# Seven-product groups for branch B's queries and keys and six gate tiles of the long sequence, in a stage of their own

## The chip, the cores and the metric

One core of one Trainium2 chip. The metric is the time of one execution on the device in microseconds (us); lower is better. The engines are PE (matmul), DVE (vector), ACT (scalar), POOL (GpSimd) and SP, which here only issues loads.

## The reference

One encoder layer on two sequences, `x_sample` (512 tokens, trunk 0) and `x_prompt` (1024 tokens, trunk 1), with a model width of 1024 and float32 throughout:

```python
xn = rmsnorm(x);  z = xn @ w_in       # q_A | k_A | v_A | q_B | k_B | v_B | gate_A | gate_B
o_A = grouped-query attention(q_A, k_A, v_A)      # 8 heads over 2 key heads, rotary, every key
o_B = neighbourhood attention(q_B, k_B, v_B)      # 8 heads, window of at most 8 x 16 on a grid 64 wide, bias
mix = (sigmoid(gate_A) * (o_A @ w_proj_a) + sigmoid(gate_B) * (o_B @ w_proj_b)) @ w_out
x = x + mix
x = x + relu(rmsnorm(x) @ w_mlp_up)**2 @ w_mlp_down
y = rmsnorm(x)
```

`w_in` has 4352 columns. Columns 768 to 1279 are q_B, 1280 to 1791 k_B, 2304 to 3327 gate_A, 3328 to 4351 gate_B.

## The kernel before

**Precision.** Every float32 product is made of three matmuls on pairs of rounded parts (`mm3`, lines 190 to 193: high x high, low x high, high x low). So each matrix that feeds PE is first split: ACT writes the high part (`hi = copy(src)`), DVE the low part (`lo = src - hi`). One product with a depth of 1024, a 128-wide weight and 512 tokens takes 8 x 3 = 24 matmuls of 128x512.

**Stages.** `run` handles a trunk: trunk 0 first, then trunk 1 with twice the tokens (`NB` = 2 blocks `tb` of 512 tokens). For each of two key-head groups g there is a stage R (norm, q/k/v of branch A, rotary) and a stage A (attention over all keys). Then branch B makes its attention (stage B), stage G merges, and after both trunks the MLP runs for all tokens. The MLP's up-projection already uses seven-product groups (tiles `ua`, `ub`, `uc`, `ud`; helper lines 1184 to 1304).

**Stage A of trunk 1** runs over 8 units (head, half of the queries) and 8 key chunks `kc`. Per chunk: four transposes into `pTs` (L722), ACT copies them to `pths` (L727), DVE subtracts into `ptls` (L728), and two chunks later PE multiplies both with the values into `os` (L698, L699). In chunks 0, 1, 3 and 4 a score tile `ss` of the next unit (L679, L680) is made: DVE takes its maximum (L682), ACT the exponential (L685), DVE the reciprocal of the sum (L687), and POOL scales (L688).

**Filling.** `gate` makes the gate tiles: a generator of steps of one `mm3` (three matmuls into `gpss`), with a weight split per tile (ACT L180, DVE L186). `fill.pull(n)` puts n such steps into the PE stream. In stage A of trunk 1 six of eight chunks pull one step; `fill.drain()` at the end of each g places what is left. Gate A's tiles 0 to 3 belong to g = 0, tiles 4 to 7 to g = 1. Gate B's eight tiles fill stage B.

**Branch B of trunk 1.** For each pair of heads `qkproj` multiplies q and k (PE `pqbs`, `pkbs`; 4 pairs x 2 x 2 tb x 24 matmuls) and writes the split results into `qBs` and `kBs` (ACT L836 and L854, DVE L838 and L856, half the partitions at a time). There are 32 units: `s_unit` (scores `sbs`, L888; POOL adds bias `rects` and mask `msks` to `bms`, L874; one DVE operation adds and takes the minimum, L891; ACT exponential, L896; DVE reciprocal, L898; POOL scale, L899), one unit later `t_unit` (transposes `ptbs`, L911; ACT `bhs`, L916; DVE `bls`, L917), another unit later `v_unit` (`obs`, L932). Up to unit 23 five or six fill steps stand in each unit; in the last eight, seven steps of the output projection of A (`ppas`).

**What sets the order.** A list scheduler places the instructions of each engine in program order as far as its costs allow, and it may move independent ones forward; each engine then runs its list in order and waits on semaphores. SBUF comes from pools: `slot` (long-lived), `rawp` (3 buffers for raw loads), and a pool per stage. PSUM tiles come from `mm` (one bank) and `big` (two).

Of the kernel before, what the change touches and what calls it, by code (L numbers as in the profile page):

```python
# [11 lines left out]
F32 = mybir.dt.float32  # L12
# [6 lines left out]
P = 128  # L19
# [42 lines left out]
def encoder(ctx: ExitStack, tc: tile.TileContext, xs, outs, w):  # L62
# [21 lines left out]
    def phase(name, bufs=2):  # L84
        return tc.tile_pool(name=name, bufs=bufs, reuse_waits="tile")
# [293 lines left out]
    def run(tr, nxt, first):  # L379
# [89 lines left out]
        def load_v(g, alloc, pin=False):  # L469
            return load_cols(win, 1792 + 256 * g, 256, f"v{N}_{g}", alloc, pin)  # L470

        early = {}
        for g in range(2):
            with phase(f"phR{N}_{g}") as ph:
                xn_of = {}
                fresh = g == 0 and tr.ready < NT
# [105 lines left out]
                for tt in range(NT):  # L582
# [67 lines left out]
                    if first and g == 0 and tt == 1:  # L650
                        load_pad()
                    if tt == NT - 2:
                        fill.add(gate(2304, zg[0], g * 4, g * 4 + 4))
                        fill.pull(1)

                if g == 0:
# [10 lines left out]
            with phase(f"phA{N}_{g}") as ph:  # L667
# [41 lines left out]
                for ui, u in enumerate(units):  # L709
                    h, qb = u  # L710
                    if first:
                        bias_row(g * 4 + ui)
                        if g == 0 and ui == 1:
                            early["a"] = load_a(1)
                        if g == 0 and ui == 2:
                            early["v"] = load_v(1, slot)
                    nxt_u = units[ui + 1] if ui + 1 < len(units) else None
                    sdone = 0
                    for kc in range(NT):
                        pt = mm(f"pT{N}_{g}_{h}_{qb}_{kc}")  # L720
                        for j in range(4):
                            nc.tensor.transpose(  # L722
                                pt[:, j * P : (j + 1) * P], PP[u, j][:, kc * P : (kc + 1) * P], ident
                            )
                        hi = ph.tile([P, 512], F32R, tag="pth", name=f"pth{N}_{g}_{h}_{qb}_{kc}", bufs=3)
                        lo = ph.tile([P, 512], F32R, tag="ptl", name=f"ptl{N}_{g}_{h}_{qb}_{kc}", bufs=3)
                        nc.scalar.activation(hi, pt, AF.Copy)  # L727
                        nc.vector.tensor_tensor(lo, pt, hi.bitcast(F32), op=ALU.subtract)  # L728
# [12 lines left out]

        mA = {}
        wp_b = []
# [44 lines left out]
        with phase(f"phB{N}") as ph:  # L788
# [24 lines left out]
            def qkproj(pr, wqk, dest):  # L813
# [4 lines left out]
                for tb in range(NB):  # L818
# [31 lines left out]
                    for e in range(2):  # L850
# [4 lines left out]
                        for os_ in (hs, ls):  # L855
                            nc.vector.tensor_tensor(  # L856
                                kT[e][os_, 1, cs], pk[hs], kT[e][hs, 0, cs].bitcast(F32), op=ALU.subtract
                            )

            qk = {}  # L860
            def s_unit(u):
                h, j = u
# [85 lines left out]
                    finish_o(o, nq, None, ph, f"B{nm}", (hi, lo, ps))  # L948

            prep(0)  # L950
            fill.add(gate(3328, zg[1]))
            wqk = load_qk(0)
            fill.pull(1)
            for _ in qkproj(0, wqk, qk):
                pass
            units = [(h, j) for h in range(8) for j in (1, 2, 0, 3)]
            n = len(units)
            LS, LV = (1, 1) if NB == 2 else (2, 1)
            qp = None
            for i in range(n + LS + LV):  # L960
                if i < n - 8:
                    f = (5 if i < LS else 2 + i % 2) if NB == 1 else 5 + (i % 3 > 0)
                else:
                    f = 3 + i % 2 if NB == 1 else 7
                if i < n:
                    s_unit(units[i])
                    if units[i][1] == 1 and units[i][0] + 1 < 8:
                        prep(units[i][0] + 1)
                    if i % 8 == 6 and i + 2 < n:
# [19 lines left out]
                if i == 3:  # L989
                    wqk = load_qk(1)  # L990
                if qp is not None and NB == 2:
                    for _ in range(NC8):
                        next(qp)
# [713 lines left out]
```

## Time and profile before

| | |
|---|---|
| three runs | 2174.45, 2174.66, 2172.08 us; median 2174.45 us |
| span of the profiled execution | 2172.2 us |
| PE busy | 2135.6 us, 98% |
| DVE, ACT, POOL busy | 1456.1, 1109.3, 349.4 us (67%, 51%, 16%) |
| granted TensorE clock | nine tenths or more in all 40 slices |

The profile has a row per group of instructions and a timeline of each. A matmul's row is longer than its share of PE's time, since matmuls overlap: the step from one start to the next is its price. Times such as 662.7 are from the start of the span. Trunk 1 stands in it as follows: stage A of g = 0 from 470.7 to 599.7, stage R to 662.7, stage A of g = 1 to 791.4, first q/k and gates to 814.6, branch B to 1094.1, stage G to 1232. Trunk 0's stage A of g = 0 is at 56.1 to 97.8 and its branch B at 186 to 293; the MLP's up-projection begins at 1238.

### The profile page before, as it was taken

The numbers are of one execution on the slowest core, as the hardware profiler recorded it, in microseconds if no ns is written. First come the engines' busy times: TensorE is split into PE (matmuls) and PEld (weight loads), VectorE is DVE, ScalarE is ACT, GpSimd is POOL, SyncE is SP. The second block draws the span as 40 slices with busy tenths as digits, with TensorE's granted clock in tenths as the row PEclk, the third lists the DMA queues.
The fourth block names the chain that finished last, engine by engine and source line by source line (L and its number), as shares of the span: only waits on it lengthen the run. The fifth ranks groups of instructions, "written<-read, shape, count | busy, mean of one in ns | idle before, by whom it ended". The sixth has DMA issues, their size and how long they took to land. (4 is left out here: it accounts for less than half of the span.)

```text
span 2172.2 us, 32392 instructions
## 1 busy us (share of the span) xinstructions
PE 2135.6 (98%) x11162; PEld 1867.9 (86%) x11162; DVE 1456.1 (67%) x2837; ACT 1109.3 (51%) x2379; POOL 349.4 (16%) x458
## 2 busy tenths in 40 slices
PE   8999999999999999999999999999999999999998
PEld 7788778888898888888888899998999988888886
DVE  6675566777756754555772777778777777769663
ACT  5654553556645744545531466656556643433452
POOL 2232210433233313322300200003000000000000
PEclk9999999999999999999999999999999999999999
DMA  5436457620122132423464656568544799788551
GB/s 166 144 104 179 137 145 249 211 71 28 45 75 86 44 92 88 125 80 110 136 195 137 202 180 195 179 226 223 158 156 155 234 347 343 224 268 290 175 194 68
DMA packets 319773, 350.94 MB, mean 162 GB/s; under 512 B 31352, under 2 KB 255224, under 8 KB 319609
## 3 DMA queue, kind: packets, MB, share of 16 engines
q1 hardware_dynamic: 277927, 279.65, 41.4%
q10 hardware_dynamic: 36002, 52.19, 6.9%
q0 software_dynamic: 5680, 17.04, 2.7%
q8 instruction: 88, 1.44, 0.3%
q14 instruction: 76, 0.62, 0.1%
HBM read 264.85 MB, written 87.88 MB: 162 GB/s over the span
## 5 line engine op out<-in xcount | busy, mean ns | idle before, releaser
L192 PE MATMUL dn<-wd,ah 128*128 128x512 f32 x624 | 243.0, 389 | 0.0
L193 PE MATMUL dn<-wd,al 128*128 128x512 f32 x624 | 243.0, 389 | 0.0
L191 PE MATMUL dn<-wd,ah 128*128 128x512 f32 x624 | 243.0, 389 | 0.0
L1184 ACT ACTIVATE ah<-ar 128x512 fp32r<-128x512 f32 x168 | 103.9, 627 | 195.1 <-PE dn L192 176.8
L1185 DVE TENSOR_TENSOR al<-ar,ah 128x512 fp32r<-128x512 f32 x168 | 115.1, 693 | 73.9 <-ACT ah L1184 66.7
L192 PEld LDWEIGHTS dn<-wd,ah 128*128 128x128 f32 x624 | 117.2, 188 | 24.4
L193 PEld LDWEIGHTS dn<-wd,al 128*128 128x128 f32 x624 | 117.2, 188 | 24.2
L191 PEld LDWEIGHTS dn<-wd,ah 128*128 128x128 f32 x624 | 117.2, 188 | 24.1
L728 DVE TENSOR_TENSOR ptls<-pTs,pths 128x512 fp32r<-128x512 f32 x160 | 107.7, 686 | 37.9 <-ACT pths L727 37.0
L727 ACT ACTIVATE pths<-pTs 128x512 fp32r<-128x512 f32 x160 | 94.1, 597 | 74.0 <-PE pTs L722 71.8
L688 POOL TENSOR_SCALAR ps<-ps,rls 128x1024 f32<-128x1024 f32 (+1 forms) x96 | 96.6, 1007 | 216.2 <-DVE rls L687 197.2
L682 DVE TENSOR_REDUCE nms<-ss 128x1 f32<-128x1024 f32 (+1 forms) x96 | 99.9, 1041 | 25.4 <-PE ss L680 25.0
L191 PE MATMUL gpss<-xs_0h,w_gs 128*128 128x512 f32 x256 | 106.2, 415 | 0.8 <-DVE rlbs L898 0.7
L685 ACT ACTIVATE ps<-ss,nms 128x1024 f32<-128x1024 f32 (+1 forms) x96 | 93.2, 972 | 22.4 <-DVE nms L682 20.0
L722 PEld LDWEIGHTS pTs<-ident,ps 128*128 128x128 f32 x640 | 78.2, 140 | 28.1 <-POOL ps L688 4.2
L193 PE MATMUL gpss<-xs_0h,w_gs 128*128 128x512 f32 x256 | 101.7, 397 | 0.0
L192 PE MATMUL gpss<-xs_0l,w_gs 128*128 128x512 f32 x256 | 101.6, 397 | 0.0
L722 PE MATMUL pTs<-ident,ps 128*128 128x128 f32 x640 | 98.9, 274 | 1.3 <-DVE ptls L728 0.6
L176 POOL TENSOR_TENSOR rs_f<-ms_f,mhalf 128x1 f32<-128x1 f32 x6 | 4.0, 667 | 590.7 <-DVE ms_f L172 590.7
L1184 ACT ACTIVATE A<-S 128x512 fp32r<-128x512 f32 x128 | 75.9, 623 | 29.4 <-DVE S L1247 22.1
L891 DVE CUSTOM_DVE_ANT_0 sbss<-sbs,bms 128x384 f32<-128x384 f32 (+1 forms) x96 | 48.6, 508 | 58.2 <-issue 34.1
L191 PE MATMUL ud<-B,A 128*128 128x384 f32 x256 | 85.8, 335 | 1.4 <-DVE c L1302 1.4
(325 smaller groups left out, 6444.8 us busy)
## 6 DMA issues: line engine op xcount, KB each, us to landing
ar<-ud SPq DMA_DIRECT2D x120, 512.0 KB
br<-in_w_mlp_down_dram SPq DMA_DIRECT2D x72, 512.0 KB
rawu<-in_w_mlp_up_dram SPq DMA_DIRECT2D x64, 512.0 KB
ud<-c ACTq DMA_DIRECT2D x128, 192.0 KB
raw_gs<-in_w_in_dram SPq DMA_DIRECT2D x32, 512.0 KB
zgs<-sgs ACTq DMA_DIRECT2D x48, 256.0 KB
ud<-cs SPq DMA_DIRECT2D x64, 192.0 KB
raw_os<-in_w_out_dram SPq DMA_DIRECT2D x16, 512.0 KB
```

The lines of the kernel that those rows point to most:

```text
L191: nc.tensor.matmul(out, ah, bh, start=start, stop=False, **kw)
L192: nc.tensor.matmul(out, ah, bl, start=False, stop=False, **kw)
L193: nc.tensor.matmul(out, al, bh, start=False, stop=stop, **kw)
L682: nc.vector.tensor_reduce(nm_, s, axis=AX.X, op=ALU.max, negate=True)
L685: nc.scalar.activation(p, s, AF.Exp, bias=nm_, accum_out=l)
L688: nc.gpsimd.tensor_scalar(p, p, rl, 1.0, op0=ALU.mult, op1=ALU.mult)
L722: nc.tensor.transpose(pt[:, j * P : (j + 1) * P], PP[u, j][:, kc * P : (kc + 1) * P], ident)
L727: nc.scalar.activation(hi, pt, AF.Copy)
L728: nc.vector.tensor_tensor(lo, pt, hi.bitcast(F32), op=ALU.subtract)
L891: nc.vector.tensor_tensor_reduce(out=sb, in0=so, in1=bm, op0=ALU.add, op1=ALU.min, scale=-1.0, scalar=3e38, accum_out=nm_)
L1184: nc.scalar.activation(hi, src, AF.Copy)
L1185: nc.vector.tensor_tensor(lo, src, hi.bitcast(F32), op=ALU.subtract)
```

## The change

In trunk 1 seven pairs of column tiles leave the places where they were made: gate A's tiles 4 to 7, gate B's tiles 6 and 7, and the four pairs of heads each of q_B and k_B. Two tiles (256 columns) of q_B or k_B, or of a gate, times 1024 tokens and a depth of 1024 form one group: a 2x2 block product that is made with seven block products instead of eight, which takes 7 x 4 x 3 = 84 matmuls of 128x512 instead of 8 x 4 x 3 = 96. With two groups of q_B, two of k_B and three of gates there are seven groups, run in a new stage S (`wide`, pool `phS`) between branch A and branch B.

- The token forms `XF` (four new ones, of 4 chunks of 128x512 each): two subtractions and an addition of high and low parts, then the split. One chunk takes POOL 2, DVE 2 and ACT 1 operations. `x_form_step` stands in stage A of g = 1, the rest in stage S.
- The weight forms (`forms`): four DVE additions or subtractions per group and seven splits (ACT and DVE), made during the group before.
- The outputs (`group`, `put`): DVE additions of the products in PSUM and SBUF; gates go through tanh to DRAM as before; q and k are split and written to DRAM (`qd`, `kd`), and `load_qkd` reads each pair back on SP's queue, 3 MB per pair (`qBs`, `kBs`), in halves of 64 partitions.
- Fill: stage A has gate A's tiles 0, 1 (g = 0) and 2, 3 and gate B's 0 (g = 1); two of eight chunks pull in g = 0, three of eight in g = 1, and what is left of g = 1 is drained at the head of stage S. Branch B has gate B's tiles 1 to 5: eight steps at its start, five per unit in the first three units, then two or three.

```diff
+        XF, x_todo = {}, []
...
+            def chunk(i, a, b, c):
+                if i not in XF:
+                    XF[i] = tuple(slot([P, 4, 512], F32R, f"xf{n_}{N}_{i}") for n_ in "hl")
+                hi, lo = (t[:, c, :] for t in XF[i])
+                (ah, al), (bh, bl) = ([t[:, c, :].bitcast(F32) for t in XF[n]] for n in (a, b))
+                de = rawp.tile([P, 2, 512], F32, tag="raw", name=f"xd{N}_{i}_{c}")
+                nc.gpsimd.tensor_tensor(de[:, 1], al, bl, op=ALU.subtract)
+                nc.vector.tensor_tensor(de[:, 0], ah, bh, op=ALU.subtract)
+                nc.gpsimd.tensor_tensor(de[:, 0], de[:, 0], de[:, 1], op=ALU.add)
+                nc.scalar.activation(hi, de[:, 0], AF.Copy)
+                nc.vector.tensor_tensor(lo, de[:, 0], hi.bitcast(F32), op=ALU.subtract)
+
+            for i, a, b in ((2, 7, 0), (1, 4, 2), (3, 4, 7), (6, 5, 1)):
+                x_todo.extend(partial(chunk, i, a, b, c) for c in range(4))
...
+        def wide(ph):
+
+            raws = {}
+            todo = [("g", 2304 + 512, 4, zg[0])]
+            todo += [(kind, off + 256 * i, 2 * i, dst) for i in range(2) for kind, off, dst in
+                     (("q", 768, qd), ("k", 1280, kd))]
+            todo += [("g", 2304 + 768, 6, zg[0]), ("g", 3328 + 768, 6, zg[1])]
...
+                def one(i):
+                    if i == 1:
+                        S[0], S[1] = st(f"S0{N}_{n}"), st(f"S1{N}_{n}")
+                        nc.vector.tensor_tensor(S[0], a21, a22, op=ALU.add)
+                        nc.vector.tensor_tensor(S[1], S[0], a11, op=ALU.subtract)
+                    if i == 3:
+                        nc.vector.tensor_tensor(a21, a11, a21, op=ALU.subtract)
+                    if i == 4:
+                        nc.vector.tensor_tensor(S[1], a12, S[1], op=ALU.subtract)
+                    src = {0: a11, 1: S.get(1), 2: S.get(0), 3: a21, 4: S.get(1), 5: a12, 6: a22}[i]
+                    t = kf([P, 2, 4, P], f"sa{N}_{n}_{i}")
+                    nc.scalar.activation(t[:, 0], src, AF.Copy)
+                    nc.vector.tensor_tensor(t[:, 1], src, t[:, 0].bitcast(F32), op=ALU.subtract)
+                    A[i] = t
...
+            def group(n, A, side):
...
+                def prod(out, i, more):
+                    for k in range(4):
+                        mm3(
+                            out, A[i][:, 0, k, :], A[i][:, 1, k, :], XF[i][0][:, k, :], XF[i][1][:, k, :],
+                            k == 0 and not more, k == 3, skip_group_check=True,
+                        )
+                    if side:
+                        for s in side.pop(0):
+                            s()
+
+                s1, s5 = k2(f"s1{N}_{n}"), k2(f"s5{N}_{n}")
+                prod(a, 0, False)
+                nc.scalar.activation(s1, a, AF.Copy)
+                if n == 0:
+                    prod(a, 5, True)
+                    put(n, 0, 0, a)
+                prod(bk, 1, False)
+                nc.vector.tensor_tensor(s1, bk, s1, op=ALU.add)
+                prod(c, 2, False)
+                nc.scalar.activation(s5, c, AF.Copy)
+                nc.vector.tensor_tensor(s5, s5, s1, op=ALU.add)
+                if n > 0:
+                    prod(d, 3, False)
+                    put(n, 1, 1, d, s5, s5)
+                prod(c, 4, True)
+                put(n, 0, 1, c, s1)
+                if n == 0:
+                    prod(d, 3, False)
+                    put(n, 1, 1, d, s5, s5)
+                prod(d, 6, True)
+                put(n, 1, 0, d, s1, s1)
+                if n > 0:
+                    prod(a, 5, True)
+                    put(n, 0, 0, a)
+
+            ask(0)
+            A = {}
+            side = forms(0, A)
+            while side or len(x_todo) > 4:
+                x_form_step()
+                for s in side[:2]:
+                    s()
+                side = side[2:]
+            ask(1)
+            fill.drain()
+            for n in range(len(todo)):
+                nA = {}
+                side = forms(n + 1, nA) if n + 1 < len(todo) else []
+                side = [[s] for s in side]
+                if n == 0:
+                    side = [[x_form_step] * 2, [x_form_step] * 2] + [[]] + side[:3] + [side[3] + side[4] + side[5] + side[6]]
+                group(n, A, side)
+                A = nA
+                ask(n + 2)
...
+            if g == 1 and NB == 2:
+                x_forms()
...
-                        fill.pull(1 if NB == 1 or kc % 4 < 3 else 0)
+                        fill.pull(1 if NB == 1 or kc % (4 - g) == 0 else 0)
+                        if NB == 2 and g == 1 and kc == 3 and ui >= 1:
+                            for _ in range(1 + (ui > 6)):
+                                x_form_step()
...
-                fill.drain()
+                if NB == 1 or g == 0:
+                    fill.drain()
...
+        if NB == 2:
+            with phase(f"phS{N}") as ph:
+                wide(ph)
...
+                hs = slice(64 * e, 64 * e + 64)
+                ls = slice(64 - 64 * e, 128 - 64 * e)
+                nc.sync.dma_start(qT[hs, e, :].bitcast(F32), qd[pr][hs, 0, :])
+                nc.sync.dma_start(qT[ls, e, :].bitcast(F32), qd[pr][hs, 1, :])
+                for os_ in (hs, ls):
+                    nc.sync.dma_start(kT[os_, :, :].bitcast(F32), kd[pr][hs, :, :])
...
+                load_qkd(0, qk, 0)
+                fill.add(gate(3328, zg[1], 1, 6))
+                fill.pull(1)
+                load_qkd(0, qk, 1)
+                fill.pull(7)
...
-                    f = (5 if i < LS else 2 + i % 2) if NB == 1 else 5 + (i % 3 > 0)
+                    f = (5 if i < LS else 2 + i % 2) if NB == 1 else (5 if i < 3 else 2 + (i % 5 < 4))
...
+                    if NB == 2:
+                        if i % 8 in (4, 7) and i + 4 < n:
+                            load_qkd(i // 8 + 1, qk, i % 8 // 7)
```

**PE in branch A of trunk 1, g = 0, head 1, between key chunks 5 and 6.** Names are those of the stage above; `gpss` is a gate step. Before:

```order
L722 MATMUL pTs_0_1_0_5_6188<-ident,ps_0_1_0_3_6009 128x128
L191 MATMUL gpss_2304_1_1_6032<-xs_1h_4989,w_gs_2304_1_5612 128x512
L192 MATMUL gpss_2304_1_1_6032<-xs_1l_4991,w_gs_2304_1_5612 128x512
L193 MATMUL gpss_2304_1_1_6032<-xs_1h_4989,w_gs_2304_1_5612 128x512
L698 MATMUL os_0_1_0_6134<-pths_0_1_0_3_6142,vhls_0_4783 128x512
L699 MATMUL os_0_1_0_6134<-ptls_0_1_0_3_6143,vhls_0_4783 128x512
L722 MATMUL pTs_0_1_0_6_6202<-ident,ps_0_1_0_0_5911 128x128
```

After (lines are shifted; L884, L885 and L908 are the former L698, L699 and L722):

```order
L908 MATMUL pTs_0_1_0_5_6156<-ident,ps_0_1_0_3_5993 128x128
L884 MATMUL os_0_1_0_6102<-pths_0_1_0_3_6110,vhls_0_4791 128x512
L885 MATMUL os_0_1_0_6102<-ptls_0_1_0_3_6111,vhls_0_4791 128x512
L908 MATMUL pTs_0_1_0_6_6167<-ident,ps_0_1_0_0_5900 128x128
L908 MATMUL pTs_0_1_0_6_6167<-ident,ps_0_1_0_1_5928 128x128
```

The gate step between the transposes of chunk 5 and the `os` matmuls of chunk 3 is gone, so the next transposes follow after two matmuls instead of five.

**DVE in branch A, g = 1, at the end of the first unit's key chunks.** `ptls`, `nms` (the maximum) and `rls` are the work of the unit; L914, L868 and L873 are the former L728, L682 and L687. Before:

```order
L728 TENSOR_TENSOR ptls_1_0_0_6_8072<-pTs_1_0_0_6_8066,pths_1_0_0_6_8071 128x512
L728 TENSOR_TENSOR ptls_1_0_0_7_8089<-pTs_1_0_0_7_8083,pths_1_0_0_7_8088 128x512
L728 TENSOR_TENSOR ptls_1_0_1_0_8100<-pTs_1_0_1_0_8094,pths_1_0_1_0_8099 128x512
L682 TENSOR_REDUCE nms_1_1_0_0_8108<-ss_1_1_0_0_8103 128x1
L728 TENSOR_TENSOR ptls_1_0_1_1_8127<-pTs_1_0_1_1_8121,pths_1_0_1_1_8126 128x512
L682 TENSOR_REDUCE nms_1_1_0_1_8135<-ss_1_1_0_1_8130 128x1
```

After, where `xds` is a difference of two token blocks and `xfls` the low part of a token form:

```order
L873 RECIPROCAL rls_1_0_1_3_7921<-ls_1_0_1_3_7919 128x1
L489 TENSOR_TENSOR xfls_1_8707<-xds_1_0_8708,xfhs_1_8706 128x512
L489 TENSOR_TENSOR xfls_1_8707<-xds_1_1_8876,xfhs_1_8706 128x512
L914 TENSOR_TENSOR ptls_1_0_0_7_7958<-pTs_1_0_0_7_7952,pths_1_0_0_7_7957 128x512
L868 TENSOR_REDUCE nms_1_1_0_0_7977<-ss_1_1_0_0_7972 128x1
L914 TENSOR_TENSOR ptls_1_0_1_0_7969<-pTs_1_0_1_0_7963,pths_1_0_1_0_7968 128x512
L486 TENSOR_TENSOR xds_1_2_8998<-xs_1h_4997,xfhs_2_8056 128x512
```

Three operations of the token forms (L486, L489) now stand among those of the unit.

**DVE at the head of stage S, first group.** `sas` is a weight form's low part, `S0s`/`S1s` sums of weight blocks, `wbs` a product in PSUM, `s1s` its sum. Nothing of the kind stood here before:

```order
L548 TENSOR_TENSOR sas_1_0_9258<-rawss_1_0_9129,sas_1_0_9258 128x512
L486 TENSOR_TENSOR xds_6_0_9193<-xs_0h_4561,xfhs_1_8706 128x512
L613 TENSOR_TENSOR s1s_0_9177<-wbs_0_9174,s1s_0_9177 128x512
L489 TENSOR_TENSOR xfls_6_9192<-xds_6_0_9193,xfhs_6_9191 128x512
L539 TENSOR_TENSOR S0s_1_9275<-rawss_1_0_9129,rawss_1_1_9131 128x512
L486 TENSOR_TENSOR xds_6_1_9199<-xs_0h_4561,xfhs_1_8706 128x512
L540 TENSOR_TENSOR S1s_1_9276<-S0s_1_9275,rawss_1_0_9129 128x512
L542 TENSOR_TENSOR rawss_1_0_9129<-rawss_1_0_9129 128x4x128
L616 TENSOR_TENSOR s5s_0_9178<-s5s_0_9178,s1s_0_9177 128x512
L489 TENSOR_TENSOR xfls_6_9192<-xds_6_1_9199,xfhs_6_9191 128x512
```

The addition from `wbs` (L613) waits for PE's second product, and token form 6 (`xds_6`, `xfls_6`) stands behind it in DVE's list.

**SP's queue at the entry of branch B.** `rects` is the bias tile of a head, `raw_bqs`, `raw_bks` and `raw_gs` are raw weights, `vss` values. Before:

```order
L216 DMA raw_bks_0_0_9265<-in_w_in_dram 128x8x128
L216 DMA raw_gs_3328_0_0_9271<-in_w_in_dram 128x8x128
L216 DMA raw_gs_3328_1_0_9462<-in_w_in_dram 128x8x128
L216 DMA raw_gs_3328_2_0_9602<-in_w_in_dram 128x8x128
L216 DMA raw_bqs_1_0_9670<-in_w_in_dram 128x8x128
L795 DMA rects_0_9240<-biases 128x768
L795 DMA rects_1_9443<-biases 128x768
```

After, `qBs` and `kBs` are read back from `qds` and `kds`:

```order
L1066 DMA kBs_0_0_10210<-kds_0_4741 64x2048 x2
L1063 DMA qBs_0_10209<-qds_0_4737 64x1024
L1064 DMA qBs_0_10209<-qds_0_4737 64x1024
L1066 DMA kBs_0_1_10221<-kds_0_4741 64x2048 x2
L989 DMA rects_0_10190<-biases 128x768
L989 DMA rects_1_10281<-biases 128x768
L995 DMA vss_1_10283<-vds_4732 32x4x128 x16
```

The two bias tiles now stand behind the read-back of the first pair's q and k.

More of the change, by code (lines that the diff above doesn't have):

```diff
@@ L652, in run @@
                     if tt == NT - 2:
-                        fill.add(gate(2304, zg[0], g * 4, g * 4 + 4))
+                        if NB == 1:
+                            fill.add(gate(2304, zg[0], g * 4, g * 4 + 4))
+                        else:
+                            fill.add(gate(2304, zg[0], g * 2, g * 2 + 2))
+                            if g == 1:
+                                fill.add(gate(3328, zg[1], 0, 1))
                         fill.pull(1)
@@ L950, in run @@
             prep(0)
[L951 to L955, printed above, removed]
+            if NB == 1:
+                fill.add(gate(3328, zg[1]))
+                wqk = load_qk(0)
+                fill.pull(1)
+                for _ in qkproj(0, wqk, qk):
+                    pass
+            else:
+                load_qkd(0, qk, 0)
+                fill.add(gate(3328, zg[1], 1, 6))
+                fill.pull(1)
+                load_qkd(0, qk, 1)
+                fill.pull(7)
             units = [(h, j) for h in range(8) for j in (1, 2, 0, 3)]
@@ L988, in run @@
                     fill.add(pa)
-                if i == 3:
+                if i == 3 and NB == 1:
                     wqk = load_qk(1)
-                if qp is not None and NB == 2:
-                    for _ in range(NC8):
-                        next(qp)
                 fill.pull(f - f // 2)
```

79 lines of the change are left out of this document (78 added, 1 removed).

## The prediction

> **What bounds the kernel now.** I read the page first: busy shares, then the slices.
>
> ```profile
> span 2172.2 us, 32392 instructions
> ...
> PE 2135.6 (98%) x11162; PEld 1867.9 (86%) x11162; DVE 1456.1 (67%) x2837; ACT 1109.3 (51%) x2379; POOL 349.4 (16%) x458
> ...
> PE   8999999999999999999999999999999999999998
> ...
> DVE  6675566777756754555772777778777777769663
> ...
> PEclk9999999999999999999999999999999999999999
> ```
>
> PE has work for 98% of the span in every slice, at a clock of nine tenths or more. So the time is PE's list, and a change pays what it removes there less the gaps that it opens. Next I asked for the busy times by stage, to see how near the other engines are. The rows below are, in order: trunk 1's stage A with g = 0 (A0) and g = 1 (A1), the first q/k and gates, branch B up to the last units; then three stages as likenesses: trunk 0's stage A and branch B, which have less fill, and the MLP's up-projection, which is already made of seven-product groups.
>
> ```profile
> core 0: us, PE busy (x) PEld busy (x) DVE busy (x) ACT busy (x) POOL busy (x), PEclk, DMA share, GB/s
> 470.70:599.70 129.00, 128.56 (x689) 104.89 (x687) 92.92 (x146) 83.80 (x148) 36.74 (x32) 1.00 0.12 37
> 662.70:791.40 128.70, 128.60 (x689) 104.95 (x687) 92.03 (x144) 84.84 (x149) 37.27 (x33) 1.00 0.17 49
> 791.40:814.60 23.20, 23.20 (x103) 18.97 (x101) 9.62 (x26) 8.41 (x13) 3.54 (x4) 1.00 0.63 175
> 814.60:1028.50 213.90, 210.50 (x1088) 175.72 (x1087) 112.84 (x317) 106.87 (x234) 61.28 (x84) 1.00 0.34 102
> 56.10:97.80 41.70, 40.66 (x202) 31.45 (x202) 32.34 (x67) 29.99 (x64) 11.90 (x16) 1.00 0.47 147
> 186.00:293.00 107.00, 101.22 (x513) 82.46 (x512) 62.10 (x190) 59.06 (x137) 25.71 (x42) 0.98 0.49 143
> 1238.00:1480.00 242.00, 240.57 (x1380) 238.46 (x1379) 185.78 (x314) 150.29 (x300) 9.72 (x15) 1.00 0.60 194
> ```
>
> In A0 PE is idle for 0.44 us of 129.00 and DVE is busy 72% of the time; in trunk 0's stage A DVE is at 78% and PE idle 1.04 us of 41.70, 2.5%. Branch B loses 3.4 us of 213.9, its likeness in trunk 0 5.8 of 107.0. The up-projection loses 1.43 of 242.00 with DVE at 77%.
>
> The price of a matmul comes from the timeline, whose rows overlap:
>
> ```profile
> 587.60 0.60 PE L722 MATMUL pTs<-ident,ps 128*128 128x128 f32 x4
> 587.96 0.48 PE L191 MATMUL gpss<-xs_1h,w_gs 128*128 128x512 f32 x1
> 588.27 0.39 PE L192 MATMUL gpss<-xs_1l,w_gs 128*128 128x512 f32 x1
> ...
> 799.79 0.39 PE L192 MATMUL pkbs<-xs_0l,w_bks 128*128 128x512 f32 x1
> ...
> 811.80 0.39 PE L191 MATMUL pkbs<-xs_1h,w_bks 128*128 128x512 f32 x1
> ```
>
> From 799.79 to 811.80 stand 54 matmuls of 128x512 without a gap, 53 steps: 12.01 / 53 = 0.2266 us each. After transposes the next step is 0.31 us (587.96 to 588.27), 0.08 more; that cost stays where it is, since no transpose goes.
>
> **The gain.** Each of the seven groups has 84 matmuls instead of 96, so PE's list loses 7 x 12 = 84 steps of 0.2266: **19.0 us**. The moved matmuls cost the same wherever they stand; only the gaps that the move opens count against this. I go through five places.
>
> **1. A0: less fill.** Two of four gate tiles leave (96 matmuls, 21.8 us), so A0 shrinks to 107.2 us if PE has no gaps. DVE's rows, by line:
>
> ```profile
> L728 DVE TENSOR_TENSOR ptls<-pTs,pths 128x512 fp32r<-128x512 f32 x160 | 107.7, 686 | 37.9 <-ACT pths L727 37.0
> L682 DVE TENSOR_REDUCE nms<-ss 128x1 f32<-128x1024 f32 x64 | 77.9, 1217 | 15.3 <-PE ss L680 15.0
> L186 DVE TENSOR_TENSOR w_gs<-raw_gs,w_gs 128x512 fp32r<-128x512 f32 x64 | 43.0, 716 | 5.4 <-ACT w_gs L180 5.2
> L687 DVE RECIPROCAL rls<-ls 128x1 f32<-128x1 f32 x96 | 15.1, 158 | 18.6 <-ACT ps L685 17.7
> L1247 DVE TENSOR_TENSOR S<-S,rawu 128x512 f32<-128x512 f32 x32 | 22.2, 692 | 1.2
> ```
>
> DVE gives up two tiles' splits (2 x 2 x 0.716 = 2.9 us) and keeps 92.92 - 2.9 = 90.0 us, 84% of 107.2. A score chunk without fill costs DVE 1.217 + 0.158 + 0.686 = 2.06 us and PE four transposes, four score matmuls and two of `os`: 0.36 + 0.08 + 6 x 0.2266 = 1.80 us. Chunks 1 and 3 of the eight units are such: 16 x 0.26 = 4.2 us if nothing is caught up; chunks 5 to 7, where DVE needs only 0.69 against PE's 0.90, catch up some. Trunk 0's share, 2.5%, gives 2.7 us. I take 2.5, from that nearest row; ends 1 and 5.
>
> **2. A1: less fill and the token forms.** 48 gate matmuls leave and 27 more are drained in stage S: 128.7 - 75 x 0.2266 = 111.7 us. DVE loses one tile's splits (1.4) and gains 14 operations of the forms (10 others go into the stage R before, where it has room, 8 into S): 92.03 - 1.4 + 14 x 0.692 = 100.3 us, 90%. They come in clusters, six in the first two units and eight in the last three. A unit has 111.7 / 8 = 14.0 us of PE and (92.03 - 1.4) / 8 = 11.3 of DVE; with four of them DVE has 14.1, as much as PE. Besides, POOL now subtracts beside DVE, and where POOL and DVE both work on two SBUF operands the trace has:
>
> ```profile
> 1211.91 1.62 POOL L327 TENSOR_TENSOR B<-ta,B 128x512 fp32r<-128x512 f32 x1 [2.85 <-DMA hn<-hnd]
> ...
> 1211.69 2.39 DVE L327 TENSOR_TENSOR B<-ta,B 128x512 fp32r<-128x512 f32 x2
> ```
>
> Two DVE operations took 2.39 us together beside one of POOL that started 0.22 us after the first, against 2 x 0.692. All twelve of this line:
>
> ```profile
> L327 DVE TENSOR_TENSOR B<-ta,B 128x512 fp32r<-128x512 f32 x12 | 13.1, 1100 | 0.0
> ```
>
> At that 1.100 us, A1's forms make 15.4 us and DVE 106.0, 95%. I take 4.5 us of gaps: 2.8 by trunk 0's share, and 1.7 (my choice) for the five crowded units; ends 2 and 8.5, the upper one the 2.8 and all of the slow operations' excess, 14 x 0.41 = 5.7.
>
> [...]
>
> **3. Stage S.** PE's list here is 7 x 84 x 0.2266 = 133.2 us plus gates. At the head 27 drained gate matmuls (6.1 us) cover DVE's first forms. In DVE's list 13 operations (9.0 us) stand between the last `os` of branch A and the addition from `wbs`, which waits for PE's second product: 6.1 + 3 x 12 x 0.2266 = 14.3 us, counting product 5 ahead of it. Then 17 more operations up to the last chunk of token form 6: 17 x 0.692 = 11.8, so 26.1 us. PE wants that chunk at 6.1 + (72 + 9) x 0.2266 = 24.5. A wait of 1.6 us, and of 4.5 if the seven form operations among them take 1.100; I take 2.8 between these. After that the up-projection's share, 0.6% of the other groups' 114 us, gives 0.7: together 3.5; ends 1 and 7.
>
> **4. Entry of branch B.** SP's list puts 3 MB of q and k ahead of the bias tile:
>
> ```profile
> rects<-biases SPq DMA_DIRECT2D x16, 384.0 KB
> ...
> msks<-in_mask_dram POOLq DMA_DIRECT2D x1, 576.0 KB, 8.2
> ```
>
> ```profile
> L874 POOL TENSOR_TENSOR bms<-rects,msks 128x384 f32<-128x384 f32 x48 | 45.5, 949 | 103.8 <-DVE nmbs L891 91.1 <-DMA msks<-in_mask_dram 7.6 <-DVE rlbs L898 5.1
> ```
>
> The slots of the first q/k become free after the last group's second product, five products (13.6 us) before the end of S. At the 175 GB/s of the window from 791.4 the 3.5 MB up to the first `rects` take 20.0 us, to 6.4 after the end of S; `bms` (0.949) and the DVE operation behind it (0.56, its row is below) end at 7.9. PE has 21 gate matmuls and then 18 more with two pairs of scores, 39 x 0.2266 + 0.7 = 9.5 us, before it wants them. The mask, asked for after the fourth product, is earlier (8.2 us in its row). So nothing is lost at 175 GB/s; at the 143 of trunk 0's branch B the loads take 24.5 and all ends at 12.4, 2.9 us too late. I take 1.5; ends 0 and 4.
>
> **5. Branch B with thin fill.** A unit before, with 18 gate matmuls, by the scores of two neighbours:
>
> ```profile
> 903.62 0.57 PE L888 MATMUL sbs<-kBs,qBs 128*128 128x384 f32 x2
> ...
> 904.94 0.63 PE L888 MATMUL sbs<-kBs,qBs 128*128 128x384 f32 x2
> ...
> 910.16 0.57 PE L888 MATMUL sbs<-kBs,qBs 128*128 128x384 f32 x2
> ...
> 905.71 0.56 DVE L891 CUSTOM_DVE_ANT_0 sbss<-sbs,bms 128x384 f32<-128x384 f32 x1 [0.49 <-issue]
> ...
> 907.25 1.16 POOL L899 TENSOR_SCALAR pbs<-pbs,rlbs 128x384 f32<-128x384 f32 x2
> ```
>
> It lasts 910.16 - 903.62 = 6.54 us. With 2.8 fill steps instead of 6 it is 6.54 - 3.2 x 0.68 = 4.36. Its chain, from the end of the second scores (905.57) through DVE, ACT and DVE to the end of POOL's pair (908.41), takes 2.84 us; the transposes of that unit come a loop later, at least 4.36 - 0.7 = 3.6 us after. It fits with 0.8 us to spare. Idle PE per unit: before 3.4 us over 24, 0.14; trunk 0, 5.8 over some 26 units, 0.22. The difference over 24 units, 2 us, is what I take; ends 0 (q/k projection's waits go, of which one is below) and 8 (a bias addition of POOL, 0.4 us more than the scale at the wrong moment, in 20 units).
>
> ```profile
> PE sbs L888 <- DVE kBs L856: 0.8, 1, 0.8
> ```
>
> **Sum.** 2.5 + 4.5 + 3.5 + 1.5 + 2 = 14.0 us of gaps against 19.0: **5.0 us faster**, 2172.2 - 5.0 = 2167.2 us of span. The median of the runs lies 2.25 us above the profiled span (2174.45 against 2172.2), and I predict for it 2174.45 - 5.0 = **2169.5 us**. About 0.2%, 4.35 us, is what a measurement here can tell from no change.
>
> **The rivals.**
> - *PE stays the bound everywhere* (0.15). All low ends: 1 + 2 + 1 + 0 + 0 = 4, so 15 faster, 2159.5. For it: 0.44 us idle in A0 and 1.43 in the up-projection. Against: DVE goes from 72% to 84 and 90% in branch A.
> - *DVE, held up by POOL, becomes the bound of A1 and of S's head* (0.22): slower. In A1 32 POOL scales and 14 POOL operations of the forms stand against 14 DVE operations with two SBUF operands; if each takes what the blocked one of the pair took, 2.39 - 0.69 = 1.70, DVE has 92.03 - 1.4 + 14 x 1.70 = 114.4 us against PE's 111.7. It decides once an operation costs over (111.7 - 90.6) / 14 = 1.5 us. A1 then loses its upper end and 2.7 on top, 11.2, and S its 7; with the rest (2.5 + 1.5 + 2) 24.2 are lost, 5.2 slower, 2179.7. For it: the two rows. Against: twelve like them averaged 1.100.
> - *Branch B starves* (0.12): `rects` late (4) and the chain 0.4 us too long in 20 units (8), with 2.5 + 4.5 + 3.5: 22.5, 3.5 slower, 2178.0; with all five at their high ends (32.5) 13.5 slower, 2188.0. Against: 0.8 us to spare.
> - *The removed matmuls come back as waits, one for one* (0.03): the groups do what the old tiles did in the time of 96, 2174.5.
> - The forecast (0.48), from 10 faster to none.
>
> **Range and chances.** The range goes from the first rival, 2159, to all high ends together, 2188. The forecast's own is 2164 to 2175. Faster by over 0.2%: 0.31 of the forecast's 0.48 and the first rival's 0.15, together 0.46. Same: 0.15 of the forecast, 0.04 and 0.02 of the second and third, 0.03 of the fourth: 0.24. Slower: 0.02, 0.18 and 0.10: 0.30.
>
> **What would show it.** Right: A0 near 110 us and A1 near 116, PE's waits there on DVE's `ptls` and on `pTs`; the groups 19 us apart with one wait on `xfls` 6 in the first; branch B's units near 4.5 us. Wrong: A1 over 121 us or form operations of over 1.5 us (second rival); PE waiting for `rects` or POOL's `pbs` in most units (third); no waits at all in A0 (first).

## The result: slower by 2.5%

The changed kernel takes 2229.77 us (median of 4 runs, 2226.96 to 2231.63), the kernel before 2173.88 us (4 runs). The ratio is 1.0252, 95% interval [1.0237, 1.0266]. The prediction was 2169.5 us, 5.0 faster, in a range of 2159 to 2188; the time lies above the range, and the change made the kernel slower.

The page of the changed kernel's profiled execution, the lines shown of before:

```profile
span 2225.2 us, 32477 instructions
...
PE 2138.9 (96%) x11078; PEld 1860.5 (84%) x11078; DVE 1515.8 (68%) x2897; ACT 1123.6 (50%) x2412; POOL 396.6 (18%) x490
...
PE   8999999899989989997799999999999999999998
...
PEclk9999999999999999998799999999999999999999
```

PE has 84 matmuls fewer (11078 against 11162) but is busy for 3.3 us longer, and in two slices, 1001 to 1112 us, its granted clock is 0.8 and 0.7. By stage, from the windows of both kernels: first before (A0, stage R of g = 1, branch B; the rows of A1 and of the first q/k stand in the prediction), then after (A0, R, A1, stage S, branch B):

```profile
470.70:599.70 129.00, 128.56 (x689) 104.89 (x687) 92.92 (x146) 83.80 (x148) 36.74 (x32) 1.00 0.12 37
599.70:662.70 63.00, 63.00 (x428) 62.21 (x426) 37.21 (x114) 25.27 (x124) 22.16 (x32) 1.00 0.27 88
...
814.60:1094.10 279.50, 275.30 (x1435) 230.37 (x1435) 160.94 (x440) 139.40 (x311) 79.82 (x108) 1.00 0.36 107
```

```profile
470.20:579.20 109.00, 107.79 (x592) 86.00 (x590) 88.01 (x142) 79.46 (x142) 36.39 (x32) 1.00 0.10 27
579.20:648.80 69.60, 66.45 (x429) 64.44 (x427) 45.46 (x121) 26.65 (x128) 37.59 (x43) 0.95 0.17 55
648.80:771.20 122.40, 114.05 (x615) 90.17 (x614) 96.56 (x154) 84.66 (x150) 56.48 (x46) 1.00 0.10 28
771.20:927.10 155.90, 148.44 (x637) 120.39 (x636) 99.37 (x166) 59.67 (x101) 13.06 (x9) 0.97 0.53 156
927.10:1147.30 220.20, 186.30 (x989) 153.94 (x988) 122.75 (x348) 106.03 (x259) 83.22 (x112) 0.89 0.63 171
```

"Without gaps" below takes the time of the stage before, less the matmuls that left, at 0.2266 us each: from branch B went 288 of the q/k projection and 159 of gates. Stage S is new; its 27 + 588 + 21 = 636 matmuls are counted at the same price.

| stage | before | after, without gaps | after | lost | predicted loss |
|---|---|---|---|---|---|
| A0 | 129.0 | 107.2 | 109.0 | 1.8 | 2.5 |
| R of g = 1 | 63.0 | 63.0 | 69.6 | 6.6 | 0 |
| A1 | 128.7 | 111.7 | 122.4 | 10.7 | 4.5 |
| first q/k, then S | 23.2 | 144.1 | 155.9 | 11.8 | 3.5 |
| branch B | 279.5 | 178.2 | 220.2 | 42.0 | 3.5 |
| sum | 623.4 | 604.2 | 677.1 | 72.9 | 14.0 |

So the list is 19 us shorter, and 73 are lost against that. Over the five stages PE is idle for 49.3 us more than before, and its matmuls take 23.6 longer than the list without gaps. What PE waited for in the changed kernel, the longest entries (total, times, longest):

```profile
PE ppas L191 <- ACT oXs L180: 12.0, 2, 10.4
PE sbs L1096 <- DMA kBs<-kds: 11.6, 2, 9.4
PE wds L191 <- DVE s5s L559: 7.1, 1, 7.1
PE sbs L1096 <- DVE nmbs L1099: 4.9, 6, 1.7
```

The first two are loads of branch B: the read-back of k, and `rawos`, from which `oXs` is split for the projection of A. The third is the head of S. `rawos` is asked for some 5 us after PE has begun to wait for `oXs` (1067.8), behind sixteen value loads:

```profile
1058.07 14.69 SPq L995 DMA_DIRECT2D vss<-vds  x16
...
1073.28 4.36 SPq L945 DMA_DIRECT2D rawos<-oads  x3
```

### The profile page after: what moved, and what is told of

Same layout as the page of the kernel before. It is cut to its first block, busy times and chain, and to the rows that moved or that the text cites. A ratio compares the mean times of both kernels' runs of the same rounds, so it can differ in the third digit from the quotient of the medians.

```text
span 2225.2 us, 32477 instructions
## 1 busy us (share of the span) xinstructions
PE 2138.9 (96%) x11078; PEld 1860.5 (84%) x11078; DVE 1515.8 (68%) x2897; ACT 1123.6 (50%) x2412; POOL 396.6 (18%) x490
## 5 line engine op out<-in xcount | busy, mean ns | idle before, releaser
L192 PEld LDWEIGHTS dn<-wd,ah 128*128 128x128 f32 x624 | 117.2, 188 | 24.1
L914 DVE TENSOR_TENSOR ptls<-pTs,pths 128x512 fp32r<-128x512 f32 x160 | 107.2, 683 | 20.1 <-ACT pths L913 19.0
L868 DVE TENSOR_REDUCE nms<-ss 128x1 f32<-128x1024 f32 (+1 forms) x96 | 99.6, 1038 | 23.2 <-PE ss L866 22.3
L908 PEld LDWEIGHTS pTs<-ident,ps 128*128 128x128 f32 x640 | 77.9, 140 | 36.5 <-POOL ps L874 12.6
L908 PE MATMUL pTs<-ident,ps 128*128 128x128 f32 x640 | 101.4, 275 | 5.9 <-POOL ps L874 4.5
L191 PE MATMUL gpss<-xs_0h,w_gs 128*128 128x512 f32 x208 | 87.9, 422 | 3.9 <-DVE vts L757 3.2
L1400 DVE TENSOR_TENSOR A<-S,A 128x512 fp32r<-128x512 f32 x128 | 84.4, 685 | 3.9 <-ACT A L1399 3.9
L191 PE MATMUL uc<-B,A 128*128 128x384 f32 x256 | 85.7, 335 | 0.0
```

What stands on the lines that cost most here:

```text
L191: nc.tensor.matmul(out, ah, bh, start=start, stop=False, **kw)
L192: nc.tensor.matmul(out, ah, bl, start=False, stop=False, **kw)
L868: nc.vector.tensor_reduce(nm_, s, axis=AX.X, op=ALU.max, negate=True)
L908: nc.tensor.transpose(pt[:, j * P : (j + 1) * P], PP[u, j][:, kc * P : (kc + 1) * P], ident)
L1400: nc.vector.tensor_tensor(lo, src, hi.bitcast(F32), op=ALU.subtract)
```

## The experiments

**Is the read-back late because of where it stands in SP's list?** SP's list in the changed kernel, around the third read-back (pair 3):

```profile
1033.17 14.53 SPq L995 DMA_DIRECT2D vss<-vds  x16
1047.86 0.45 SPq L1063 DMA_DIRECT2D qBs<-qds  x1
1048.36 0.60 SPq L1064 DMA_DIRECT2D qBs<-qds  x1
1049.05 3.73 SPq L1066 DMA_DIRECT2D kBs<-kds  x2
```

Sixteen value loads take SP 14.5 us, and only then comes the read-back that PE wants at 1049.2. Ahead of the value loads (L995) SP's longest waits are, as the profile infers them, for other transfers to land, loads (`kBs`) and stores (`obds`, `zgs`):

```profile
SPq L995 <- DMA kBs<-kds: 14.8, 5, 5.8
SPq L995 <- DMA obds<-os_Bs: 13.6, 9, 2.3
SPq L995 <- DMA zgs<-sgs: 12.1, 3, 5.0
```

In the first experiment the read-back goes ahead of the value loads:

```diff
-                    if units[i][1] == 1 and units[i][0] + 1 < 8:
-                        prep(units[i][0] + 1)
                     if NB == 2 and i % 8 in (4, 7) and i + 4 < n:
                         load_qkd(i // 8 + 1, qk, i % 8 // 7)
+                    if units[i][1] == 1 and units[i][0] + 1 < 8:
+                        prep(units[i][0] + 1)
```

> Edit: in branch B the read-back of the next pair's q and k is issued ahead of a head's bias and value loads, so in SP's list it stands before the 16 value loads instead of behind them. Theory SP (the read-back is late because SP issues one load after another and each waits for an earlier one to land): PE's two waits for kBs (11.6 us in all) go, with the refill of the chain and the slower clock behind them; branch B falls from 220 to about 200 us, the time from 2229.8 to about 2210. The wait for oXs (12.0 us) stays. Rival bandwidth (the 3 MB per pair are too much however they are ordered): the value loads or the bias become late instead, 2225 to 2230.

Measured: 2229.09 us, branch B 223.0. The wait moved, as the rival said:

```profile
PE sbs L1096 <- DMA vss<-vds: 12.2, 1, 12.2
PE ppas L191 <- ACT oXs L180: 11.5, 2, 9.8
...
PE sbs L1096 <- DMA kBs<-kds: 3.2, 1, 3.2
```

So another place in the same list does not help. Whether it is the list or the bytes, the next run tells.

```diff
-                nc.sync.dma_start(qT[hs, e, :].bitcast(F32), qd[pr][hs, 0, :])
+                nc.gpsimd.dma_start(qT[hs, e, :].bitcast(F32), qd[pr][hs, 0, :])   # and the others of load_qkd
```

> Edit: the read-back of q and k is issued from POOL's queue instead of SP's; order in the program unchanged. Theory SP: SP's list loses 24 large loads, so kBs, the values and oXs all come in time; branch B about 185 us, the time about 2195. Rival bandwidth: no change beyond 5 us, 2225 to 2230. Rival POOL: POOL waits at those loads for their buffers and its scales and bias additions come late; PE waits for pbs and bms in most units, 2220 or more.

Measured: 2204.76 us, 25 less; branch B 195.2 with the same bytes at a higher rate, and no wait for kBs, oXs or values among its longest:

```profile
926.90:1122.10 195.20, 180.49 (x989) 152.00 (x988) 119.07 (x346) 104.70 (x258) 95.86 (x136) 0.96 0.73 193
```

193 GB/s against 171, and a DMA share of 0.73 against 0.63: over the whole stage the DMA engines had room, and SP's list did not. (In stretches of the changed kernel they were busy throughout: a share of 0.97 from 1009 to 1024, and of 1.01 from 1050 to 1068, where the late loads came together.) The rival of the bytes falls for these 25 us. PE's waits for POOL's `pbs` are 1.4 us against 3.8; its longest wait left is 6.7 us for `nmbs` at the entry. Branch B still loses 17.0 us against its time without gaps.

**And the thin fill?** Here pairs 1 to 3 are not read back at all, and every head uses the first pair's q and k; the list of PE is unchanged.

```diff
-                        if i % 8 in (4, 7) and i + 4 < n:
-                            load_qkd(i // 8 + 1, qk, i % 8 // 7)
+                        if i % 8 == 4 and i + 4 < n:
+                            qk[i // 8 + 1] = qk[0]
```

> Leaves out the read-back of pairs 1 to 3: all heads use the first pair's q and k. Same PE list, same fill, 9 MB less on SP's queue. Theory read-back (branch B's 42 us are the loads' doing): B falls from 220 to about 190 with only the entry's wait left, the time about 2200. Rival thin fill (the units are too short for their chain): B stays over 205 us, with waits for pbs and nmbs in most units; 2215 or more.

Measured: 2194.71 us, and branch B

```profile
932.20:1113.90 181.70, 175.45 (x989) 148.91 (x988) 120.95 (x348) 105.89 (x259) 86.17 (x112) 0.99 0.51 154
```

3.5 us over the 178.2 without gaps. So 38.5 of branch B's 42.0 us hang on the read-back of three pairs; the thin units and the first pair cost 3.5. The other queue won back 25.0 of the 38.5; what makes up the rest was not taken apart (with the read-back go its 9 MB, its entries in SP's list and its buffers).

**The token forms.** Left out: the products use existing token blocks in their place, and PE's list is unchanged.

```diff
-            def chunk(i, a, b, c): ...
+            XF[2], XF[1], XF[3], XF[6] = XF[0], XF[4], XF[7], XF[5]
```

> Leaves out the four token forms: the products use existing token blocks in their place, so PE's list is the same but DVE, POOL and ACT lack the 16 chunks. Theory forms (they are what was lost in stage R, A1 and the head of S): R of g = 1 back from 69.6 to 63 us, A1 from 122.4 to about 114, stage S from 155.9 to about 146; the time 2229.8 - 25 = about 2205. Rival fill (A1 loses because PE has less to fill with): A1 stays over 119 us, only the 7.1 us wait at the head of S and the stage R are won; about 2215.

Measured: 2195.27 us. Stage R and A1:

```profile
582.00:645.40 63.40, 63.40 (x429) 62.36 (x428) 36.16 (x113) 24.47 (x124) 21.90 (x32) 1.00 0.34 102
645.40:757.00 111.60, 111.13 (x610) 89.43 (x609) 86.89 (x138) 80.55 (x142) 36.00 (x32) 1.00 0.07 21
```

A1 is at its time without gaps: less fill alone costs nothing there, and all 10.7 us are the forms, as the 6.6 of stage R. S did not gain as expected (158.8 us): PE is busy for all of its first 59.0 us, so the wait at its head is gone, but others came later in it (4.2 us for `s5s`, 3.2 for `s1s`). Branch B fell to 200.1, which neither theory had said. The forms and the value tiles come from the same pool (`slot`), and without the forms SP begins its value loads 24.1 us ahead of branch B (891.74 against 915.8), in the changed kernel 2.9 us behind its start (930.01 against 927.1). That the forms' buffers hold back the loads was not tried by itself; these 20 us and the 38.5 above overlap.

**Why do the forms cost so much?** In the changed kernel, at the head of S, first POOL's and then DVE's timeline:

```profile
783.74 1.68 POOL L485 TENSOR_TENSOR xds<-xs_0l,xfls 128x512 f32<-128x512 f32 x1 [13.06 <-DVE sas L548]
```

```profile
784.18 1.79 DVE L486 TENSOR_TENSOR xds<-xs_0h,xfhs 128x512 f32<-128x512 f32 x1
785.89 0.68 DVE L613 TENSOR_TENSOR s1s<-wbs,s1s 128x512 f32<-128x512 f32 x1
```

DVE's subtraction began 0.44 us after POOL's, ended 0.55 after it, and took 1.79 us instead of some 0.68; the next one (L613), which began 0.22 us ahead of POOL's next operation (786.11), took 0.68. Two opposite edits on top of the read-back from POOL's queue: all of the forms on DVE, or all but the last operation on POOL.

```diff
-                nc.gpsimd.tensor_tensor(de[:, 1], al, bl, op=ALU.subtract)
+                nc.vector.tensor_tensor(de[:, 1], al, bl, op=ALU.subtract)      # the addition too
```

> Edit on top of the read-back from POOL's queue (2204.8 us): the token forms' two POOL operations run on DVE. Theory port (POOL and DVE block each other in the forms): an operation that reads two SBUF operands is back at 0.69 us, stage R back to about 64 us, the wait at the head of S falls from 7.1 to under 3 us, A1 to about 118; about 2190. Rival load (A1 has no room on DVE for any of it): DVE gets two more operations a chunk, A1 rises to 128 or more; about 2205 or slower.

```diff
-                nc.vector.tensor_tensor(de[:, 0], ah, bh, op=ALU.subtract)
+                nc.gpsimd.tensor_tensor(de[:, 0], ah, bh, op=ALU.subtract)
```

> Edit on top of the read-back from POOL's queue (2204.8 us): the third subtraction of a token form, so far on DVE, runs on POOL; DVE keeps one operation a chunk. Theory port: the POOL operations are more and still block DVE's remaining one and each other; stage R and A1 no better (68 and 124 us or more), head of S worse, since a chunk is three POOL operations of 1.3 to 1.7 us in a row; about 2210. Rival load: A1 gains what DVE loses, 7 operations of 0.7 to 1.8, to about 117; about 2198.

Measured: 2189.66 us with DVE alone, 2217.19 with POOL. On DVE alone stage R, A1 and S are

```profile
579.30:642.50 63.20, 63.20 (x427) 62.24 (x426) 43.48 (x126) 25.64 (x126) 23.75 (x32) 1.00 0.19 59
642.50:760.90 118.40, 112.91 (x615) 90.40 (x614) 105.65 (x170) 85.73 (x151) 38.91 (x32) 1.00 0.10 29
760.90:909.10 148.20, 146.82 (x636) 118.20 (x635) 100.82 (x180) 61.13 (x102) 4.76 (x9) 1.00 0.56 163
```

against 68.3, 125.2 and 155.8 with the same read-back: 19.5 us won in these stages, and 15.1 in the whole time (2204.76 to 2189.66), by giving DVE 32 operations more. The same line's operation before and after the edit (mean ns), in the changed kernel and with DVE alone:

```profile
L486 DVE TENSOR_TENSOR xds<-xs_0h,xfhs 128x512 f32<-128x512 f32 x4 | 7.1, 1772 | 0.0
```

```profile
L486 DVE TENSOR_TENSOR xds<-xs_0h,xfhs 128x512 f32<-128x512 f32 x4 | 2.7, 684 | 0.0
```

With more on POOL, R rises to 73.7 us and S to 160.2. That DVE and POOL hold each other up holds for these operations: at the head of S a subtraction took DVE 1.75 to 1.79 us beside POOL, and POOL 1.64 to 1.68 beside DVE. Why they do, by a port as the theory's name has it or otherwise, no run shows. How much of the 19.5 us is that, and how much the shorter chain (an operation that takes POOL 1.28 us by itself takes DVE 0.68), the two runs do not separate. A1 keeps losing 6.7 us on DVE alone; PE's waits there are 2.6 us for `kTs`, 2.1 for POOL's `ps` and 0.7 for DVE's `ptls`. The edit without the other read-back:

> Edit: the changed kernel with the token forms on DVE alone; read-back from SP as in the change. Theory (forms and read-back are separate costs): the 15 to 19 us that the same edit won beside the other read-back, 2229.8 - 17 = about 2213; branch B still about 220 us. Rival (the earlier S lets the loads run earlier too, as in the run without forms): branch B 200 to 205, about 2197.

Measured: 2210.54 us, branch B 218.6. The costs add, nearly: forms on DVE win 19.2 us beside SP's read-back and 15.1 beside POOL's. Branch B does not gain from an S that is done earlier.

**Can fill be moved to the waits?** One gate tile into S's first group, or 12 steps from the units to the entry of branch B, both beside the read-back from POOL's queue.

```diff
+                    fill.pull(8)          # group 0 of S, ahead of product 3; the tile's other steps ahead of product 6
```

> Edit on top of the read-back from POOL's queue (2204.8 us): one gate tile of B (48 matmuls, 10.9 us) is made inside the first group of S, where PE waits 7.1 us; branch B's units get two fill steps, sometimes three. Theory clock (PE loses the wait and then runs at a lower clock, together 12 us): S grows by only some 1 us instead of 10.9, and branch B shrinks by 10.9 less what its thinner units lose (2 to 4); about 2197. Rival (the wait is moved behind the gate tile, since the forms are late by themselves): S grows by 8 or more; 2204 or slower.

```diff
-                fill.pull(7)
+                fill.pull(19)             # and three, then two or three steps per unit
```

> Edit on top of the read-back from POOL's queue (2204.8 us): 19 instead of 7 fill steps before branch B's first unit, fewer in the units. Theory entry (the 6.8 us wait and the lower clock behind it come from the bias tiles being late after S): the wait falls by 8 us of cover, B from 195 to about 188; about 2198. Rival thin fill: the units lose as much as the entry wins, within 2 us of 2204.8.

Measured: 2217.72 and 2208.33 us, both slower than 2204.76, so neither theory holds. With the gate tile in it S grew by 9.4 us: its waits became shorter, 2.2 us at the longest, but PE is still idle there for 5.0 us against 7.5. And branch B, with 48 matmuls fewer, took 197.1 instead of 195.2. Its waits there:

```profile
PE sbs L1099 <- DVE nmbs L1102: 13.0, 9, 7.7
PE ptbs L1122 <- POOL pbs L1110: 11.6, 8, 6.4
```

At the entry 12 steps (8.2 us) more made the stage ahead 7.9 us longer and branch B 8.9 shorter, so together 1.0 is won there; that the whole time is 3.6 us longer comes from elsewhere (S begins 6.7 us later in this trace, behind stages that the edit leaves alone). The longest wait for `nmbs` fell from 6.7 to 2.0 us, yet branch B still loses 16.3 us against its shorter list, where it lost 17.0. Taking the gate tile's steps out of the units returned nothing.

**The entry.** On top of forms on DVE and the read-back from POOL's queue, the first head's bias tile gets a raw buffer and is asked for early, from POOL's queue (the other heads keep the line marked with a minus):

```diff
-                rc = ph.tile([P, 16, 48], F32, tag="rect", ...);  nc.sync.dma_start(rc, ...)
+                rc = rawp.tile([P, 1024], F32, tag="raw", ...)    # head 0 only;  nc.gpsimd.dma_start(rc, ...)
```

> Edit on top of forms on DVE and read-back from POOL's queue (2189.7 us): the bias tile of the first head lies in a raw buffer and is asked for from POOL's queue, so it needs no memory of stage S. Theory entry (PE waits 7.0 us at branch B's second unit because the bias tile is asked for at 915.7, behind value loads that wait for buffers): the wait falls to under 2 us and the slower clock behind it goes; B from 195 to about 186, the time about 2181. Rival (values or mask are as late): the wait stays over 5 us, 2187 or more.

Measured: 2189.03 us against 2189.66, branch B 195.2 against 195.0. The wait fell (7.0 to 2.8 us at the longest) and nothing was won by it: what else holds the entry stays open.

**Gates alone**, as in the change and with the forms on DVE:

```diff
-            todo += [(kind, off + 256 * i, 2 * i, dst) for i in range(2) ...]     # qkproj stays in branch B
```

> Edit: only the three gate groups are made as seven products; q and k of branch B are projected as before, without DRAM. PE loses 36 matmuls (8.2 us) instead of 84. Theory read-back (branch B's loss comes from q and k through DRAM): branch B loses nothing against before; R, A1 and the head of S lose some 29 us as in the changed kernel; 2173.9 - 8.2 + 29 = about 2195. Rival thin fill (branch B is slow because few gate steps are left between its units): branch B loses 20 us or more here too, 2215 or more.

> Edit: only the three gate groups as seven products (q and k as before, no DRAM), and the token forms on DVE alone. The gates-only run had 2201.1 us; forms on DVE took 5.1 from stage R, 6.7 from A1 and 7.6 from S. Theory (the costs of forms and read-back are separate): 2201.1 - 19.4 = about 2182. Rival (they share a cause, such as the slots): 2190 or more.

Measured: 2201.08 and 2180.87 us. Branch B takes 248.3 us in both; 279.5 less 144 gate matmuls is 246.9, so it loses 1.4 when q and k stay on chip. With gates alone the time is 6 us over the 2195 that were expected, which was not traced further. The second is the best of all: 1.0028 times the kernel before [1.0018, 1.0038], still slower.

## Why the prediction was wrong

- **The gain** was right: 84 matmuls fewer, 19.0 us by their price.
- **Steps 4 and 5, branch B, failed.** They priced the first pair's read-back and the chain of a thin unit, 1.5 and 2. The run without pairs 1 to 3 loses 3.5 us, the same sum, which does not show that each of the two terms was right. The step that failed is step 5: it followed a unit's chain from `sbs` to POOL's pair as if q and k were there. The three other pairs, 9 MB in SP's list between value loads, had no term at all: 38.5 us. The rival "branch B starves" had the place right and the cause and size wrong (12 us, by `rects` and the chain).
- **Step 2, A1**: 10.7 for 4.5, and split the wrong way. The 2.8 for less fill were nothing; the forms cost all of it. They did not do it through the sum of DVE's time, by which I judged: DVE is busy for 96.56 of 122.40 us, and its form operations there averaged 0.68 to 0.87 us, below the 1.100 of my upper end. PE's longest waits in A1:

```profile
PE pTs L908 <- POOL ps L874: 3.5, 4, 1.1
PE ss L865 <- ACT kTs L734: 2.5, 1, 2.5
```

  The second stands at A1's head. In ACT's list `kTs` came behind a form's `xfhs`, and that waited for POOL's form operation:

```profile
651.11 0.63 ACT L488 ACTIVATE xfhs<-xds 128x512 fp32r<-128x512 f32 x1 [2.71 <-POOL xds L487]
651.65 0.26 ACT L734 ACTIVATE kTs<-pqs 128x128 fp32r<-128x128 f32 x1
```

- **Step 2 also let ten form operations go into stage R "where it has room"**: 6.6 us. DVE's busy share there was 59% before, but the stage is a chain. Rows of POOL, then of DVE and PE, from stage R:

```profile
632.00 3.31 POOL L485 TENSOR_TENSOR xds<-xs_1l,xs_0l 128x512 f32<-128x512 f32 x2 [2.88 <-ACT xfhs L488]
635.28 1.80 POOL L485 TENSOR_TENSOR xds<-xs_1l,xfls 128x512 f32<-128x512 f32 x1
637.05 1.17 POOL L176 TENSOR_TENSOR rs_As<-ms_As,mhalf 128x5 f32<-128x5 f32 x1
```

```profile
638.25 1.05 DVE L806 SCALAR_TENSOR_TENSOR ts<-zs,rs_As,gtab 128x64 f32<-128x64 f32 x5 [2.32 <-POOL rs_As L176]
640.14 0.96 DVE L489 TENSOR_TENSOR xfls<-xds,xfhs 128x512 fp32r<-128x512 f32 x1 [0.84 <-ACT xfhs L488]
...
641.49 0.79 PE L191 MATMUL gpss<-xs_0h,w_gs 128*128 128x512 f32 x1 [3.15 <-DVE vts L757]
```

  Three form operations stood ahead of `rs_As`, the norm's factor, and DVE waited for it; a fourth, `xfls`, stood in DVE's list ahead of `vts`, for which PE waited 3.15 us, the only wait of this stage.
- **Step 3, the head of S**: 11.8 for 3.5. A wait was foreseen at this place, of 1.6 to 4.5 us by up to 1.100 an operation, but for `xfls` 6. It was 7.1 us, and for DVE's addition `s5s` (L559), which came in DVE's list behind form operations. Their subtractions took 1.77 us there, about the 1.70 that only the second rival used.
- **Step 1, A0**, 1.8 for 2.5, was right in size. Its reason is not shown: PE's longest waits there are for POOL's `ps` (0.7 us in all), not for DVE's `ptls`, and A1 lost nothing by less fill alone.
- **No step had the clock.** Behind the longer waits PE ran slower, at a granted clock of 0.50. From S, behind the 7.1 us (rows of the timeline):

```profile
802.93 0.79 PE L191 MATMUL wds<-xfhs,sas 128*128 128x512 f32 x1 [7.14 <-DVE s5s L559]
...
805.65 0.63 PE L191 MATMUL wds<-xfhs,sas 128*128 128x512 f32 x1
806.08 0.63 PE L192 MATMUL wds<-xfls,sas 128*128 128x512 f32 x1
```

  One step is 0.43 us there, against 0.2266, for twelve steps or 5 us, which costs 2.5 us more. In R fourteen such steps, or 6 us, behind the 3.15 us cost 3.0 more. The granted clock is 0.50 from 803.0 to 807.7 in S and from 641.5 to 647.0 in R, and 1.00 from 808.2 to 815.0. In branch B PE is idle for 33.9 us, 29.7 more than before, and its matmuls take 12.3 us longer, at a granted clock of 0.89. At A1's head the clock stayed at 1.00 behind a wait of 2.5 us (651.6 to 656.0); how long a wait has to be to lower it, and for how long, the runs do not show.

What the second rival rests on, DVE held up by POOL, is shown at the head of S (1.77 us an operation against 0.68 with DVE alone). In A1 its condition, over 1.5 us an operation, was not met (0.68 to 0.87 by line), though A1 passed the 121 us that I had named as its sign. R, A1 and S together lost 29.1 us, of which the forms on DVE alone won back 19. They are the smaller part.

## What to carry to other kernels

When a tile goes through DRAM instead of staying on chip, price every load of it in the queue that issues it, with what stands there already; moving 32 loads to another queue was worth 25 us here with the bytes unchanged. A low busy share (59% of DVE in stage R before) is no room where the stage is a chain: look at who waits for the operation behind which the new one is put. A wait of some microseconds on PE can cost more than itself: here 3.15 us cost 3.0 more and 7.1 us 2.5 more at the lower clock, 0.50.

## What the runs showed of the hardware

- A float32 subtraction of 128x512 with two SBUF operands takes DVE 0.68 us alone and, in the four at the head of S, 1.77 beside POOL (POOL: 1.28 alone, up to 1.80 beside DVE). Splitting such work over both engines was 15 to 19 us slower here than DVE alone.
- 16 value loads of 64 KB took SP 7.8 to 12.0 us in branch B before and, but for the first 16, 12.0 to 17.4 in the changed kernel. They stayed long with the read-back on POOL's queue (9.3 to 16.4) and without pairs 1 to 3 (9.1 to 14.0), so the loads of 512 KB between them in the list are not the whole reason.
- After a wait of 7.1 us PE's step was 0.43 instead of 0.23 us for some 5 us, after one of 3.15 us for some 6, at a granted clock of 0.50.
